# A hybrid decoder layer on one core: two token blocks turned on VectorE, token scales sent through DRAM, one weight split moved

## The chip, the cores and the metric

The kernel runs on one core of one Trainium2 chip. A core has TensorE (PE, with its weight loads PEld), VectorE (DVE), ScalarE (ACT), GpSimd (POOL) and SyncE (SP), each with its own in-order queue; SP issues nearly all the DMAs here, and 16 DMA engines carry them out. The metric is the device time of one execution in microseconds (us). All arithmetic is float32, with matmuls in three passes over operands that are split in a high and a low part (`fp32r`).

## What is computed

One decoder layer over 1024 tokens of width 1024, with a mixer of two kinds of heads and a feed-forward part:

```
h = rmsnorm(x, mix_pre_norm)
proj = h @ w_in
q_a, k_a, v_a, q_h, f_h, i_h, g_h = split(proj)
attn = rmsnorm(dilated_mixture_attention(q_a, k_a, v_a, slopes), attn_out_norm)
rec = hgrn2_recurrence(q_h, f_h, i_h, g_h, lower_bounds, hgrn_out_norm)
x = x + rmsnorm(concat([attn, rec]) @ w_out, mix_post_norm)
h = rmsnorm(x, mlp_pre_norm)
x = x + rmsnorm(square(relu(h @ w_ff1)) @ w_ff2, mlp_post_norm)
```

The root mean square of a token is one number per token. The kernel therefore multiplies the unscaled, gain-weighted `x` with `w_in` and puts the token's scale (`rstd0`) on the products afterwards.

## The kernel before

The work around the change is the first 60 us. The token dimension is cut into eight blocks of 128 tokens (`xr0` to `xr7`), the width into eight slices of 128 (`k`). The order of the work is written out by hand: instructions stand on each engine in the order in which the code issues them, and SP issues DMAs in that order too. At most eight of SP's DMAs are under way at once, since each one reuses the semaphore of the DMA eight before it and waits for that one to land.

**Turning x.** Matmuls need `x` with the width on the partitions. `x_turn` (L284) transposes pieces of 128 by 128 on PE into PSUM (L289), then ACT writes the high part `hTh` with the gain as scale (L290) and DVE the low part `hTl` (L291). `x_mm` multiplies the turned pieces with the first head's two weight slabs `wig0` (i and gate columns), three passes each (L90 to L92), into four PSUM banks `pig_0` to `pig_3`, which hold the blocks in the pairs (0, 1), (2, 4), (3, 5), (6, 7). The main loop goes over groups of blocks: groups[2] is blocks 2 and 3, groups[3] is 4 and 5, groups[4] is block 6, groups[5] is block 7. While group `i` is multiplied, group `i + 1` is turned, so each slice `k` of loop step 3 has one transpose of block 6, and each slice of step 4 one of block 7.

**Token scales.** `squares` (L300) sums the squares of a block's tokens on ACT; `rsqrt_mean` (L82, L83) makes `rstd0` on POOL, for blocks 0 to 5 after step 3 and for blocks 6 and 7 after step 4. `ig_evac` (L263 on ACT, L264 on DVE) empties a bank and scales it: one block's `inat` on ACT, then its `gate` on DVE; the second `inat` of a bank waits for the first `gate`.

**The query weights.** `w_split` (L86 on ACT, L87 on DVE) takes the next raw slab from the stream of weights, splits it into `wh` and `wl`, and issues the load of a later slab. The first head's query slab is `raw2`, its forget slab `raw3`. In the kernel before, `raw2` is split after step 4, between the emptying of `pig_0` and of `pig_1`; `raw3` is split when all four banks are empty.

**The rows of scales.** Query and forget products have tokens on the free dimension, so they need the scales as a row, the same on every partition (`rrow`). `row_scale` (L302) makes 512 of them at a time: four transposes on PE of a broadcast column (L307), and a copy on ACT (L308). It is called for each half from `hgrn_qf`, behind the query matmuls `pm_q` of that half; then DVE multiplies `pm_q` by `rrow` (L441). The bank of `pm_q` is then free for the forget matmuls `pm_f`. `pm_q` and `pm_f` take their banks in turn from the two that held `pig_0` and `pig_1`.

Between `ig_evac` and L441, DVE also makes masks and bounds (L383 to L389), ACT loads another table and computes the sigmoid of the gates (L268), and DVE multiplies with it (L269).

A later part of the kernel (L1163, L1205) already loads pieces of 128 rows as squares of 32 by 32 and turns them with DVE's transpose.

Of the kernel before, what the change touches and what calls it, by code (L numbers as in the profile page):

```python
# [8 lines left out]
F32 = mybir.dt.float32  # L9
F32R = mybir.dt.float32r  # L10
U8 = mybir.dt.uint8
AF = mybir.ActivationFunctionType
ALU = mybir.AluOpType
# [4 lines left out]
P = 128  # L18
T = 1024
D = 1024  # L20
NK = D // P
# [11 lines left out]
def f32(ap):  # L33
    return ap.bitcast(F32)
# [3 lines left out]
def hymba_layer(ctx, tc, x, w_in, w_out, w_ff1, w_ff2, g_pre, lb_logits, g_mix, g_post,  # L38
                g_mlp, g_mlp_post, bias_tab, level_masks, ident_in, fold_in, out):
    nc = tc.nc  # L40
    V, S, G, TE = nc.vector, nc.scalar, nc.gpsimd, nc.tensor
# [8 lines left out]
    dp = ctx.enter_context(tc.tile_pool(name="spill", bufs=1, space=DRAM))  # L50

    def slab(tag, name, dtype=F32, shape=(P, T)):
        return sp.tile(list(shape), dtype, tag=tag, name=name,
                       bufs={"S": 9, "T": 9, "P": 3, "BT": 2, "V8": 2, "R": 1}[tag])

    def bank(tag, name):
        return ps.tile([P, 512], F32, tag=tag, name=name,
                       bufs={"mm": 2, "s": 2, "t": 2, "pv": 2}[tag])
# [4 lines left out]
    def col(name, n=1):  # L63
        return tp.tile([P, n], F32, tag=f"c{n}", name=name)

    ident = cp.tile([P, P], F32, name="ident")
    own = cp.tile([P, 6, 32], U8, name="own")
    near = cp.tile([P, 3, 32], U8, name="near")
    gpre = cp.tile([P, NK], F32, name="gpre")
# [5 lines left out]
    rstd0 = cp.tile([P, NT], F32, name="rstd0")  # L75
# [4 lines left out]
    def rsqrt_mean(dst, ssum, n, width):  # L80
        t = col("ms", width)
        G.tensor_scalar(t, ssum, 1.0 / n, EPS, op0=ALU.mult, op1=ALU.add)  # L82
        G.tensor_tensor(out=dst, in0=t, in1=nhalf[:, :width], op=ALU.pow)  # L83

    def split_into(hi, lo, src, eng=V):
        S.activation(hi, src, AF.Copy)  # L86
        eng.tensor_tensor(out=lo, in0=src, in1=f32(hi), op=ALU.subtract)  # L87

    def three_pass(dst, lhs, rhs, start, stop):
        TE.matmul(dst, lhs[0], rhs[0], start=start, stop=False)  # L90
        TE.matmul(dst, lhs[0], rhs[1], start=False, stop=False)  # L91
        TE.matmul(dst, lhs[1], rhs[0], start=False, stop=stop)  # L92
# [10 lines left out]
    def w_load():  # L103
        i = done[0]
        if i < len(stream):
            raws[i] = wp.tile([P, T], F32, tag="raw", name=f"raw{i}", bufs=2)
            nc.sync.dma_start(out=raws[i], in_=stream[i][0])
            done[0] += 1

    def w_split(eng=V):  # L110
        i = done[1]
        if i < len(stream):
            if done[0] <= i:
                w_load()
            hl = stream[i][1]
            if hl is None:
                hl = (wp.tile([P, T], F32R, tag="wh", name=f"wh{i}", bufs=2),
                      wp.tile([P, T], F32R, tag="wl", name=f"wl{i}", bufs=2))
            else:
                hl = hl()  # L120
            raw = raws.pop(i)
            if WO0 <= i < W10:
                gain = gcols[:, i - WO0:i - WO0 + 1]
                S.activation(hl[0], raw, AF.Copy, scale=gain)
                eng.scalar_tensor_tensor(hl[1], raw, gain, f32(hl[0]), op0=ALU.mult, op1=ALU.subtract)
            else:
                split_into(hl[0], hl[1], raw, eng)
            parts[i] = hl
            done[1] += 1
            w_load()  # L130
# [95 lines left out]
    def part_tok(blk, k, t0, n=1):  # L226
        c = (t0 % 4) * P
        return tuple(blk[q, k // 4, t0 // 4][:, k % 4, c:c + n * P] for q in "hl")
# [8 lines left out]
    def x_load(t):  # L237
        nc.sync.dma_start(out=xrows[t], in_=x[t * P:(t + 1) * P, :])
# [4 lines left out]
    x_load(0)  # L243
    for _ in range(2):
        w_load()
    for t in range(1, NT):
        x_load(t)
    V.memset(f32(ones), 1.0)
    V.memset(nhalf, -0.5)
    rrow = slab("R", "rrow")  # L250
# [5 lines left out]
    pick32 = cp.tile([P, 32], F32, name="pick32")  # L256
    mix_dram = dp.tile([T, AW], F32, name="mixd")
    rec_dram = dp.tile([T, AW], F32, name="recd")
    x2_dram = [dp.tile([P, D], F32, name=f"x2d{t}") for t in range(NT)]

    def ig_evac(hd, pm, blocks):
# [21 lines left out]

    def x_turn(t0, n, k):  # L284
        hi, lo = part_tok(hT, k, t0, n)
        pt = bank("t" if turned[0] % 2 else "s", f"xt{t0}_{k}")[:, :n * P]
        turned[0] += 1
        for j in range(n):
            TE.transpose(pt[:, j * P:(j + 1) * P], xrows[t0 + j][:, k * P:(k + 1) * P], ident)  # L289
        S.activation(hi, pt, AF.Copy, scale=gpre[:, k:k + 1])  # L290
        V.scalar_tensor_tensor(lo, pt, gpre[:, k:k + 1], f32(hi), op0=ALU.mult, op1=ALU.subtract)  # L291

    def x_mm(t0, n, k):
        for t in range(t0, t0 + n):
            three_pass(place[t], part_tok(hT, k, t), ig_view(wig[0], k), k == 0, k == NK - 1)
# [4 lines left out]
            S.activation(dump, xrows[t], AF.Square, accum_out=ssq0[:, t:t + 1])  # L300

    def row_scale(hf):  # L302
        sl = slice(hf * 512, hf * 512 + 512)
        pt = bank("t", f"rb{hf}")
        for j in range(4):
            t = hf * 4 + j
            TE.transpose(pt[:, j * P:(j + 1) * P], rstd0[:, t:t + 1].to_broadcast([P, P]), ident)  # L307
        S.activation(rrow[:, sl], pt, AF.Copy)  # L308

    def keep_warm(n, w=256):  # L310

# [46 lines left out]
    for i, grp in list(enumerate(groups))[1:]:  # L358
        for k in range(NK):
            if i == 2 and k < LAG:  # L360
                x_turn(*grp, NK - LAG + k)
            if i == 1 and k < LAG:
                x_turn(*grp, NK - LAG + k)
            if i == 1 and k >= LAG:
                x_turn(*groups[2], k - LAG)
            elif 1 < i < len(groups) - 1:
                x_turn(*groups[i + 1], k)
            x_mm(*grp, k)
            if i in (2, 3) and k % 3 == 1:
                squares(3 * (i - 2) + k // 3, 1)  # L370
        if i == 3:
            rsqrt_mean(rstd0[:, :6], ssq0[:, :6], D, 6)
        if i == 4:
            ig_evac(heads[0], pms0[0], PAIRED[0])
            w_split()
            ig_evac(heads[0], pms0[1], PAIRED[1])
            squares(6, 2)
            rsqrt_mean(rstd0[:, 6:], ssq0[:, 6:], D, 2)
    for q in (2, 3):
        ig_evac(heads[0], pms0[q], PAIRED[q])  # L380
    w_split()
# [48 lines left out]
    def hgrn_qf(h):  # L430
        hd = heads[h]
        box = [None]
        w = w_get(4 * h + 2)
        qt = hd["qt"] = slab("S", f"qt{h}")
        sig = slab("P", f"sig{h}")
        for hf in range(2):
            sl = slice(hf * 512, hf * 512 + 512)
            yield from proj_t(w, f"q{h}", hf, box)
            if h == 0:
                row_scale(hf)  # L440
            V.tensor_tensor(out=qt[:, sl], in0=box[0], in1=rrow[:, sl], op=ALU.mult)  # L441
            S.activation(sig[:, sl], qt[:, sl], AF.Sigmoid)
            V.tensor_tensor(out=qt[:, sl], in0=qt[:, sl], in1=sig[:, sl], op=ALU.mult)
            yield 650.0
        w = w_get(4 * h + 3, 0)
        hd["prod"] = prod = [slab("BT", f"pr{q}{h}", F32R) for q in "hl"]
        kt = hd["kt"] = slab("S", f"kt{h}")
        tot = hd["tot"] = slab("S", f"tot{h}")
        for hf in range(2):
            sl = slice(hf * 512, hf * 512 + 512)  # L450
            for n, cost in enumerate(proj_t(w, f"f{h}", hf, box)):
                if hf == 0 and n == 3:
                    w_get(4 * h + 3, 2 if h + 1 < HH else 1)
                yield cost
            fr = half(f"fr{h}{hf}")
            V.tensor_tensor(out=fr, in0=box[0], in1=rrow[:, sl], op=ALU.mult)
            S.activation(tot[:, sl], fr, AF.Sigmoid)
            S.activation(kt[:, sl], fr, AF.Sigmoid, scale=-1.0)
            V.tensor_scalar(tot[:, sl], tot[:, sl], omlb[:, h:h + 1], lb[:, h:h + 1], op0=ALU.mult, op1=ALU.add)
            V.tensor_scalar(kt[:, sl], kt[:, sl], omlb[:, h:h + 1], None, op0=ALU.mult)  # L460
            full = half(f"pr{h}{hf}")
            V.tensor_tensor(out=full, in0=qt[:, sl], in1=kt[:, sl], op=ALU.mult)
            S.activation(prod[0][:, sl], full, AF.Copy)
            V.tensor_tensor(out=qt[:, sl], in0=qt[:, sl], in1=tot[:, sl], op=ALU.mult)
            V.tensor_tensor(out=prod[1][:, sl], in0=full, in1=f32(prod[0][:, sl]), op=ALU.subtract)
            if h == HH - 1 and hf == 0:
                rrow_by_class(0)
            yield 650.0
# [925 lines left out]
    for s in range(n_steps):  # L1394
        hd, i = divmod(s, 8)
# [18 lines left out]
        kind, g = ITEMS[i]  # L1414
# [746 lines left out]
    scale, base = gpre, lbl.rearrange("p h l -> p (h l)")  # L2161
# [95 lines left out]
    for i in range(4):  # L2257
        t = 4 + i
# [15 lines left out]
        lo, hi = slice(0, 256), slice(256, 512)  # L2274
# [84 lines left out]
```

## Time and profile before

| | |
|---|---|
| median of 3 runs | 1188.24 us (1188.04 to 1188.32) |
| the profiled execution | 1189.14 us |
| its span, from the first to the last instruction | 1187.1 us |
| granted TensorE clock, mean | 0.998 |
| PE busy | 1176.2 us, 99% of the span |
| DVE busy | 845.5 us, 71% |
| ACT busy | 549.6 us, 46% |
| moved by DMA | 175.50 MB, 148 GB/s |

The profile shows one execution. Times in its rows are us from the start of the span. A timeline row has the start, the duration, the engine, the line, the operation, output and inputs by the program's names without numbers (so `pig` is any of the four banks), shapes, how many were merged into the row, and in brackets the idle time before it and what ended it. The chain that ended last is followed back from the last instruction: at each step to what released it. Busy times of PE overlap, since matmuls are pipelined: how fast PE goes is read from the distance of two starts.

### The profile page before, as it was taken

The page shows a single profiled execution, that of the slowest core. Times are in us where ns is not written, and L with a number is a line of the kernel's source. Part 1 is how long each engine was busy: PE and PEld are TensorE (multiplying, and loading weights), DVE is VectorE, ACT ScalarE, POOL GpSimd, SP SyncE. Part 2 cuts the span into 40 slices and gives each one's busy share as a digit, 9 for nine tenths or more (in the row PEclk, how much of TensorE's full clock was granted, in tenths as well). Part 3 has the DMA queues.
Part 4 walks back from the last instruction along what each step waited for, and adds up shares of the span by engine and source line. Part 5 has one row for each costly group of instructions (what it writes and reads, how often), then busy time and mean ns, then how long its engine had stood idle before and what let it go on. Part 6 is the DMA issues. An engine that isn't in the chain of part 4 may idle for free.

```text
span 1187.1 us, 17573 instructions
## 1 busy us (share of the span) xinstructions
PE 1176.2 (99%) x6454; PEld 1002.0 (84%) x6454; DVE 845.5 (71%) x1436; ACT 549.6 (46%) x1082; POOL 294.5 (25%) x282
## 2 busy tenths in 40 slices
PE   9999999999999999999999999999999999999997
PEld 9898989878888888888888888888888888888886
DVE  5696969686766678587697676675686653588796
ACT  7633334343566677765654222222244544434562
POOL 0112122001111110252503775657540000000022
PEclk9999999999999999999999999999999999999999
DMA  5222323137454555472425465554587524433337
GB/s 221 68 68 89 98 86 98 49 102 183 117 137 103 157 133 138 118 220 100 169 90 204 159 221 184 182 177 169 194 331 271 178 89 157 162 94 101 110 104 284
DMA packets 106774, 175.50 MB, mean 148 GB/s; under 512 B 31680, under 2 KB 59712, under 8 KB 106688
## 3 DMA queue, kind: packets, MB, share of 16 engines
q1 hardware_dynamic: 106544, 174.37, 46.4%
q8 instruction: 51, 0.84, 0.3%
q14 instruction: 35, 0.29, 0.1%
q10 hardware_dynamic: 144, 0.00, 0.0%
HBM read 116.91 MB, written 47.99 MB: 139 GB/s over the span
## 4 chain that ended last, share of the span: by engine, by line
PE 90%; DVE 4%; ACT 3%; issue 1%; POOL 0%; DMA 0%; DVEq 0%; POOLq 0%; ACTq 0%
PE f L2099 18%; PE f2s L2099 7%; PE pig L90 2%; PE pig L92 2%; PE pig L91 2%; PE pwo L90 2%; PE pwo L92 2%; PE pwo L91 2%; PE pm_ak L90 1%; PE pm_ak L92 1%; PE pl L537 1%; PE pm_ak L91 1%; PE pm_av L90 1%; PE pm_av L92 1%; PE pm_q L90 1%
## 5 line engine op out<-in xcount | busy, mean ns | idle before, releaser
L87 DVE TENSOR_TENSOR al<-ar,ah 128x1024 fp32r<-128x1024 f32 x56 | 70.6, 1262 | 80.7 <-ACT ah L86 78.4
L2099 PE MATMUL f<-bh,ah 128*128 128x512 f32 x320 | 124.5, 389 | 0.0
L2099 PE MATMUL f<-bl,ah 128*128 128x512 f32 x320 | 124.5, 389 | 0.0
L2099 PE MATMUL f<-bh,al 128*128 128x512 f32 x320 | 124.5, 389 | 0.0
L86 ACT ACTIVATE ah<-ar 128x1024 fp32r<-128x1024 f32 x56 | 59.2, 1056 | 86.8 <-DMA ar<-actd 86.4
L2099 PEld LDWEIGHTS f<-bh,ah 128*128 128x128 f32 x320 | 60.1, 188 | 12.6
L2099 PEld LDWEIGHTS f<-bl,ah 128*128 128x128 f32 x320 | 60.1, 188 | 12.5
L2099 PEld LDWEIGHTS f<-bh,al 128*128 128x128 f32 x320 | 60.1, 188 | 12.3
L2173 POOL TENSOR_SCALAR lbl<-ssq 128x1 f32<-128x1 f32 x4 | 3.3, 820 | 245.8 <-ACT fd L2169 245.6
L1722 POOL TENSOR_TENSOR e<-x,e 128x512 f32<-128x512 f32 x14 | 21.6, 1542 | 130.9 <-DVE x L1673 123.7
L2099 PE MATMUL f2s<-bh,al 128*128 128x512 f32 (+1 forms) x128 | 48.9, 382 | 0.0
L2099 PE MATMUL f2s<-bl,ah 128*128 128x512 f32 (+1 forms) x128 | 48.9, 382 | 0.0
L2099 PE MATMUL f2s<-bh,ah 128*128 128x512 f32 (+1 forms) x128 | 48.9, 382 | 0.0
L711 POOL TENSOR_SCALAR tout<-traw 128x256 f32<-128x256 f32 x16 | 18.9, 1180 | 101.1 <-DMA traw<-in_bias_tab_dram 98.5
L87 DVE TENSOR_TENSOR bl<-br,bh 128x1024 fp32r<-128x1024 f32 x32 | 40.1, 1254 | 0.6 <-ACT bh L86 0.5
L2116 ACT ACTIVATE acc<-f 128x512 f32<-128x512 f32 x28 | 16.7, 598 | 49.4 <-PE f L2099 49.4
L86 ACT ACTIVATE bh<-br 128x1024 fp32r<-128x1024 f32 x32 | 33.6, 1050 | 3.6 <-PE f L2099 2.3
L759 POOL TENSOR_TENSOR kl<-kf,kh 64x512 fp32r<-64x512 f32 x12 | 16.2, 1353 | 74.8 <-ACT kh L758 71.3
L90 PE MATMUL pwo<-woh,mt 128*128 128x512 f32 x80 | 32.2, 403 | 0.0
L87 DVE TENSOR_TENSOR wl<-raw,wh 128x1024 fp32r<-128x1024 f32 x21 | 25.7, 1224 | 8.6 <-ACT wh L86 8.6
L92 PE MATMUL pwo<-woh,mt 128*128 128x512 f32 x80 | 31.3, 391 | 0.0
L91 PE MATMUL pwo<-wol,mt 128*128 128x512 f32 x80 | 31.2, 390 | 0.0
(1727 smaller groups left out, 3886.5 us busy)
## 6 DMA issues: line engine op xcount, KB each, us to landing
ar<-actd SPq DMA_DIRECT2D x56, 512.0 KB, 3.6
br<-in_w_ff_dram SPq DMA_DIRECT2D x16, 1024.0 KB, 6.1
raw<-in_w_in_dram SPq DMA_DIRECT2D x28, 512.0 KB, 4.1
w1r<-in_w_ff_dram SPq DMA_DIRECT2D x14, 1024.0 KB, 6.4
actd<-e SPq DMA_DIRECT2D x17, 768.0 KB, 4.2
actd<-e SPq DMA_DIRECT2D x11, 1024.0 KB, 4.1
xr<-in_x_dram SPq DMA_DIRECT2D x8, 512.0 KB, 8.4
raw<-in_w_out_dram SPq DMA_DIRECT2D x8, 512.0 KB, 4.5
```

The lines of the kernel that those rows point to most:

```text
L86: S.activation(hi, src, AF.Copy)
L87: eng.tensor_tensor(out=lo, in0=src, in1=f32(hi), op=ALU.subtract)
L90: TE.matmul(dst, lhs[0], rhs[0], start=start, stop=False)
L91: TE.matmul(dst, lhs[0], rhs[1], start=False, stop=False)
L92: TE.matmul(dst, lhs[1], rhs[0], start=False, stop=stop)
L537: TE.matmul(pl[a:b, n, :96], kt[:, (4 * u + n) * P + a:(4 * u + n) * P + b], qs[:, :, 32 * g:32 * g + 32], start=True, stop=True, skip_gro ...
L711: G.tensor_scalar(by_class(dst[:, part_ * w:(part_ + 1) * w]), in_blocks(raw[:, FAR * DIL:]), 8.0, None, op0=ALU.mult)
L759: G.tensor_tensor(out=kl[a:b], in0=src, in1=f32(kh[a:b]), op=ALU.subtract)
L1722: eng[0].tensor_tensor(out=e1[:, 3], in0=a21, in1=e1[:, 2], op=ALU.add)
L2099: TE.matmul(pm, a[:, j, c], b[:, j, d], start=start and j == 0 and q == 0, stop=stop and j == 1 and q == 2, skip_group_check=True)
L2116: S.activation(acc_at(p, i), pm, AF.Copy)
L2173: G.tensor_scalar(base[:, t:t + 1], sums[j][:, t:t + 1], 1.0 / D, EPS, op0=ALU.mult, op1=ALU.add)
```

## The change

It has three parts.

- Blocks 6 and 7 of `x` are loaded a second time, each by four DMAs, into `xsq6` and `xsq7`, as squares: row `r` of square (a, k, g) is 32 numbers of `x`, 128 bytes, put on partition 32g + r. A `V.transpose` over 128 by 1024 turns every 32 by 32 square in place, after which the tile holds what the PE transposes of the block gave. `x_turn` for these two blocks then reads the tile instead of PSUM, and PE does nothing for it. The plain loads of blocks 6 and 7, which `squares` needs, come after the new loads on SP's queue.
- `row_scale` no longer uses PE and ACT: one DMA writes 512 scales to DRAM, a second reads them back as a row on every partition. It is called when the scales are made, after steps 3 and 4.
- `w_split` of the query slab is called at the end of step 3, and no longer between the emptying of two banks after step 4.

```diff
+    SQUARED = (6, 7)
+    xsq = {t: slab("T", f"xsq{t}") for t in SQUARED}
     for t in range(1, NT):
+        if t in SQUARED:
+            src = x[t * P:(t + 1) * P, :].rearrange("(a r) (k g f) -> g r k a f", a=4, g=4, f=32)
+            for g in range(4):
+                nc.sync.dma_start(out=xsq[t][32 * g:32 * g + 32].rearrange("p (k a f) -> p k a f", k=NK, a=4), in_=src[g])
+        else:
+            x_load(t)
+    for t in SQUARED:
         x_load(t)
...
     def x_turn(t0, n, k):
         hi, lo = part_tok(hT, k, t0, n)
+        if t0 in SQUARED:
+            piece = xsq[t0][:, k * P:(k + 1) * P]
+            S.activation(hi, piece, AF.Copy, scale=gpre[:, k:k + 1])
+            V.scalar_tensor_tensor(lo, piece, gpre[:, k:k + 1], f32(hi), op0=ALU.mult, op1=ALU.subtract)
+            return
...
     def row_scale(hf):
-        sl = slice(hf * 512, hf * 512 + 512)
-        pt = bank("t", f"rb{hf}")
-        for j in range(4):
-            t = hf * 4 + j
-            TE.transpose(pt[:, j * P:(j + 1) * P], rstd0[:, t:t + 1].to_broadcast([P, P]), ident)
-        S.activation(rrow[:, sl], pt, AF.Copy)
+        nc.sync.dma_start(out=rstd_dram[hf].rearrange("(t p) -> p t", p=P), in_=rstd0[:, 4 * hf:4 * hf + 4])
+        nc.sync.dma_start(out=rrow[:, 512 * hf:512 * hf + 512], in_=rstd_dram[hf].partition_broadcast(P))
...
             x_mm(*grp, k)
+            if (i, k) in ((2, 6), (3, 2)):
+                V.transpose(xsq[4 + i], xsq[4 + i])
...
         if i == 3:
             rsqrt_mean(rstd0[:, :6], ssq0[:, :6], D, 6)
+            row_scale(0)
+            w_split()
         if i == 4:
             ig_evac(heads[0], pms0[0], PAIRED[0])
-            w_split()
             ig_evac(heads[0], pms0[1], PAIRED[1])
             squares(6, 2)
             rsqrt_mean(rstd0[:, 6:], ssq0[:, 6:], D, 2)
+            row_scale(1)
...
             yield from proj_t(w, f"q{h}", hf, box)
-            if h == 0:
-                row_scale(hf)
```

DVE's queue from block 7's low parts to the second weight split, before. In the names, `xt7_4` is slice 4 of block 7, `wl2` and `wl3` are the low parts of the query and the forget slab, and `pig0_1` is the bank `pig_1`:

```order
L291 SCALAR_TENSOR_TENSOR hTl11_96<-xt7_4_535,gpre_80,hTh11_95 128x128
L291 SCALAR_TENSOR_TENSOR hTl11_96<-xt7_5_542,gpre_80,hTh11_95 128x128
L291 SCALAR_TENSOR_TENSOR hTl11_96<-xt7_6_549,gpre_80,hTh11_95 128x128
L291 SCALAR_TENSOR_TENSOR hTl11_96<-xt7_7_556,gpre_80,hTh11_95 128x128
L264 TENSOR_SCALAR gate0_144<-pig0_0_145,rstd0_86 128x128 x2
L87 TENSOR_TENSOR wl2_568<-raw2_200,wh2_567 128x1024
L264 TENSOR_SCALAR gate0_144<-pig0_1_146,rstd0_86 128x128 x2
L264 TENSOR_SCALAR gate0_144<-pig0_2_147,rstd0_86 128x128 x2
L264 TENSOR_SCALAR gate0_144<-pig0_3_148,rstd0_86 128x128 x2
L87 TENSOR_TENSOR wl3_617<-raw3_202,wh3_616 128x1024
```

The same place now, from the first square transpose on:

```order
L381 STREAM_TRANSPOSE xsq6_118<-xsq6_118 128x1024
L306 SCALAR_TENSOR_TENSOR hTl11_96<-xt4_7_417,gpre_80,hTh11_95 128x256
L299 SCALAR_TENSOR_TENSOR hTl01_94<-xsq6_118,gpre_80,hTh01_93 128x128 x3
L381 STREAM_TRANSPOSE xsq7_119<-xsq7_119 128x1024
L299 SCALAR_TENSOR_TENSOR hTl01_94<-xsq6_118,gpre_80,hTh01_93 128x128
L299 SCALAR_TENSOR_TENSOR hTl11_96<-xsq6_118,gpre_80,hTh11_95 128x128 x4
L87 TENSOR_TENSOR wl2_507<-raw2_211,wh2_506 128x1024
L299 SCALAR_TENSOR_TENSOR hTl01_94<-xsq7_119,gpre_80,hTh01_93 128x128 x4
L299 SCALAR_TENSOR_TENSOR hTl11_96<-xsq7_119,gpre_80,hTh11_95 128x128 x4
L274 TENSOR_SCALAR gate0_155<-pig0_0_156,rstd0_86 128x128 x2
L274 TENSOR_SCALAR gate0_155<-pig0_1_157,rstd0_86 128x128 x2
```

The split `wl2` has moved from between the gates of two banks to ahead of block 7's eight low parts, and two transposes over 128 by 1024 have come into the queue. ACT's queue has moved alike: `wh2` stands between the squares of block 5 and block 7's eight high parts.

SP's queue from the load of block 5 on, now:

```order
L238 DMA xr5_107<-in_x_dram 128x1024
L252 DMA xsq6_118<-in_x_dram 32x32x32 x4
L252 DMA xsq7_119<-in_x_dram 32x32x32 x4
L238 DMA xr6_108<-in_x_dram 128x1024
L238 DMA xr7_109<-in_x_dram 128x1024
L261 DMA lbl_81<-in_lb_logits_dram 128x8
L262 DMA mraw_138<-in_level_masks_dram 128x448
L107 DMA raw2_211<-in_w_in_dram 128x1024
L107 DMA raw3_213<-in_w_in_dram 128x1024
L318 DMA rstdd_145<-rstd0_86 128x4x1
L319 DMA rrow_137<-rstdd_145 128x512
L107 DMA raw4_510<-in_w_in_dram 128x1024
```

The eight loads of squares are the second and third row; before, `xr6` stood directly behind `xr5`. The two DMAs of the first row half stand ahead of the load of `raw4` (half of the second head's `wig1`); those of the second half follow it, ahead of `raw5`.

More of the change, by code (lines that the diff above doesn't have):

```diff
@@ L258, in hymba_layer @@
     rec_dram = dp.tile([T, AW], F32, name="recd")
+    rstd_dram = dp.tile([2, 4 * P], F32, name="rstdd")
     x2_dram = [dp.tile([P, D], F32, name=f"x2d{t}") for t in range(NT)]
```

## Prediction

> **What bounds the kernel now.** I read the page first: the busy times, and the chain that ended last.
>
> ```profile
> PE 1176.2 (99%) x6454; PEld 1002.0 (84%) x6454; DVE 845.5 (71%) x1436; ACT 549.6 (46%) x1082; POOL 294.5 (25%) x282
> PE 90%; DVE 4%; ACT 3%; issue 1%; POOL 0%; DMA 0%; DVEq 0%; POOLq 0%; ACTq 0%
> ```
>
> PE carries 90% of the chain, DVE and ACT 7%, DMA none. So a microsecond less on PE counts, except where the chain leaves PE. All edits lie in the first 55 us, so I followed the chain there, in order of time.
>
> ```profile
> 34.80 0.12 PE xt L289
> 34.94 0.38 ACT hTh L290
> 35.34 0.35 DVE hTl L291
> 35.70 0.27 DVE gate L264
> ...
> 36.36 0.95 ACT wh L86
> 37.37 1.11 issue
> 38.48 0.35 DVE gate L264
> ...
> 39.12 2.19 ACT sq L300 x4
> ...
> 41.67 0.71 POOL rstd L83
> ...
> 43.56 0.95 ACT wh L86
> ...
> 49.87 0.61 DVE qt L441
> 50.52 0.50 PE pm_f L90
> ```
>
> This is the part that decides. At 34.80 the chain leaves PE with block 7's last transpose, and it comes back only at 50.52, with the first forget matmul `pm_f`. In between lie the emptying of the banks, the query split `wh` with the wait for its DVE half (36.36 to 38.48), the squares, the second scales, the forget split and the masks. Only then does DVE read `pm_q` (L441) and free the bank for `pm_f`. PE is busy all that time, but it isn't what the end waits for. The waits of PE say the same with a small number, since PE has just enough work to cover the chain:
>
> ```profile
> PE pm_f L90 <- DVE qt L441: 0.3, 1, 0.3
> PEld pm_q L92 <- DVE wl L87: 0.4, 1, 0.4
> ```
>
> **The change part by part.** First what PE loses, from its timeline around the removed rows.
>
> ```profile
> 31.36 0.27 PE L289 MATMUL xt<-ident,xr 128*128 128x128 f32 x1
> 31.83 0.27 PE L289 MATMUL xt<-ident,xr 128*128 128x128 f32 x1
> ...
> 35.10 0.28 PE L90 MATMUL pig<-wig0h,hTh 128*128 128x256 f32 x1
> 35.45 0.28 PE L90 MATMUL pig<-wig0h,hTh 128*128 128x256 f32 x1
> ...
> 43.75 0.60 PE L307 MATMUL rb<-ident,rstd 128*128 128x128 f32 x4
> 44.10 0.48 PE L90 MATMUL pm_q<-hTh,wh 128*128 128x512 f32 x1
> ...
> 49.66 0.60 PE L307 MATMUL rb<-ident,rstd 128*128 128x128 f32 x4
> ```
>
> A slice with a transpose takes 0.47 (31.36 to 31.83), without one 0.35, so sixteen transposes are worth 16 x 0.115 = 1.84 us. The scales' transposes take 0.35 (43.75 to 44.10) and 0.86 (49.66 to 50.52, the 0.3 of waiting in it). The wait for `wl` is 0.4. The sum on PE is 3.45 us. With it PE would be at `pm_f` at 49.66 - 1.84 - 0.35 - 0.4 = 47.07 instead of 50.52. How much of that is kept depends on when DVE and ACT have the bank free.
>
> So the chain has to be built anew. These are ACT's rows at its start, then the durations of one operation by shape, then DVE's rows and one ACT row of the forget split.
>
> ```profile
> 24.60 1.05 ACT L300 ACTIVATE sq<-xr 128x1024 f32<-128x1024 f32 x1
> ...
> 25.64 0.62 ACT L290 ACTIVATE hTh<-xt,gpre 128x128 fp32r<-128x128 f32 x2
> ```
>
> ```profile
> L290 ACT ACTIVATE hTh<-xt,gpre 128x128 fp32r<-128x128 f32 x32 | 10.5, 366 | 5.9 <-PE xt L289 5.2
> L983 ACT ACTIVATE pd<-pd,stat 128x128 f32<-128x128 f32 x8 | 3.1, 391 | 1.0 <-DVE stat L930 1.0
> L1205 DVE STREAM_TRANSPOSE row<-row 128x512 f32<-128x512 f32 x4 | 2.8, 704 | 0.0
> ```
>
> ```profile
> 26.04 0.61 DVE L291 SCALAR_TENSOR_TENSOR hTl<-xt,gpre,hTh 128x128 fp32r<-128x128 f32 x2 [0.81 <-ACT hTh L290]
> 37.34 1.23 DVE L87 TENSOR_TENSOR wl<-raw,wh 128x1024 fp32r<-128x1024 f32 x1 [0.59 <-ACT wh L86]
> 41.59 0.35 DVE L264 TENSOR_SCALAR gate<-pig,rstd 128x128 f32<-128x128 f32 x1 [1.98 <-ACT inat L263]
> ```
>
> ```profile
> 43.46 1.05 ACT L86 ACTIVATE wh<-raw 128x1024 fp32r<-128x1024 f32 x1
> ```
>
> ACT begins block 6 at 25.64, as now, and no longer waits for PE's pace. From there its queue is full: eight high parts, three squares (blocks 3 to 5), `wh`. A high part from PSUM steps by 0.25 (0.62 for two less one of 0.37); from SBUF I add 0.03, the difference of the means 391 and 366: 0.28. A square with its read steps by 1.04 (24.60 to 25.64). So `wh` starts at 25.64 + 8 x 0.28 + 3 x 1.04 = 31.00 and ends at 32.05. DVE's `wl` steps by 1.14 (37.34 to 38.48): block 7's low parts run from 33.2, eight by 0.26 (0.61 for two), and the first gate of `pig_0` comes at 35.30. From the first gate of two banks to ACT's next other operation took 43.46 - 41.59 = 1.87, about 0.15 of it waiting for the scales (41.67 + 0.71 = 42.38). So ACT comes to the squares of blocks 6 and 7 at 35.30 + 1.72 = 37.0, where it came at 39.12. From there on the chain has the same steps as before: gain 2.1 us. The split leaving this stretch is worth the 2.1 us from 36.36 to 38.48; block 7's low parts end only 0.3 earlier, since `wl` now stands ahead of them. `pm_f` starts at 48.4; PE, which is there at about 47.4 (it waits some 0.3 for `pig_0`'s gates first), waits 1.0 us. Of the 3.45 us on PE, 1.35 are not kept. The copies L308 that ACT loses are worth nothing: ACT waits for L441 there.
>
> The square transposes are hidden. Over 1024 columns one takes 1.2 to 1.4 us, at most twice the 704 ns for 512. The first must start by about 24.2 to be done when ACT is at 25.64; the second by 30.4, before ACT reaches block 7 at 31.95. Beyond that, each microsecond costs one. What they wait for are the loads:
>
> ```profile
> 0.00:5.00 5.00, 3.39 (x9) 2.57 (x10) 0.13 (x3) 1.49 (x2) 0.69 (x6) 1.00 0.62 192
> 5.00:10.00 5.00, 5.00 (x28) 4.80 (x29) 3.99 (x12) 4.33 (x12) 0.00 (x0) 1.00 1.02 415
> 426.00:428.00 2.00, 2.00 (x12) 1.69 (x11) 1.07 (x5) 1.71 (x4) 0.00 (x0) 1.00 0.99 156
> ```
>
> ```profile
> erows<-recd SPq DMA_DIRECT2D x8, 128.0 KB, 3.2
> swd<-stat SPq DMA_DIRECT2D x8, 2.0 KB, 3.6
> gcols<-in_g_mix_dram SPq DMA_DIRECT2D x1, 4.0 KB, 5.6
> gpost<-in_g_post_dram SPq DMA_DIRECT2D x1, 512.0 KB, 3.8
> ```
>
> The windows' last columns are DMA share and GB/s. The queue has moved 0.96 + 2.08 = 3.04 MB at 10 us; the eight loads ahead of the squares are 4.19 MB, so they end at 12.8. Eight loads of just this form, `erows` (128 KB, pieces of 128 bytes), kept the DMA engines full at 156 GB/s from 426 to 428. So 1.05 MB take 6.7 us and end at 19.5, landed by 22: `xsq6`, being the first half, with some 5 us to spare, `xsq7` with 8. The loads pushed back (`xr6`, `xr7`, masks, `raw2`, 1.8 MB at 415 GB/s) end by 24; the first wanted is `raw2`, at 31.0. Price zero; at the row's other bound, 4-byte pieces, see the third rival.
>
> A rule speaks against such loads. The Trainium skill (VectorE: DVE Perf Modes, section "The three transpose paths") calls a plain DMA that transposes by strides 19 times slower than the hardware's own transposing DMA, and tells authors to turn 128 by 128 pieces on TensorE. By that rule the loads would take an estimated 48 us, and the sum would be a loss near 30 us. The row above measures 2.7 times the plain rate's time and not 19, for a load that keeps 32 numbers together, so I keep the row's price.
>
> The scales' way through DRAM: the second half is made at 42.38 - 2.1 = 40.3. A write of 512 pieces lies between `swd` (3.6) and `gcols` (5.6, pieces of 4 bytes too), the broadcast read is nearest to `gpost` (3.8, twice the size), its issue 0.4. I take 3.6 + 3.8 + 0.4: landed at 48.1. DVE's second L441 wants it at 49.7:
>
> ```profile
> 51.78 0.69 DVE L441 TENSOR_TENSOR qt<-pm_q,rrow 128x512 f32<-128x512 f32 x1
> ```
>
> 1.6 us to spare, price zero; at 5.6 twice, 2.2 us late. SP waits inside these pairs, with `raw4` and `raw5` queued behind; both are wanted only for `wig1`, behind this L441. The first half is made some 8 us before the second and wanted 2 us before it, so it has more room.
>
> **The sum.** 1189.14 of the profiled execution less 2.1 is 1187.0. The median of the runs lies 0.9 below the profiled one: 1188.24 - 2.1 = 1186.1. Steps of 0.25 to 0.30 for the sixteen short ones on ACT and DVE before the gate, and 0.2 for the transposes, put the gain at 1.4 to 2.8: 1185.4 to 1186.8. About 0.2% (2.4 us) is what a measurement can tell from no change here; the forecast is just inside, and a third of its range beyond.
>
> **The rivals.**
> 1. The chain on DVE and ACT is shorter than I build it, and PE keeps all that is taken from it: `pm_f` at 47.1, gain 3.45, 1184.8. For it: PE has 90% of the chain. Against it: between 34.80 and 50.52 the chain has no PE row.
> 2. The gain is eaten at the second row half. Landing 2.2 us late (both trips at `gcols`' 5.6), it holds DVE's L441 and all behind it: `wig1`'s split, the forget rows. At most the 2.1 us go: 1188.2. Against it: `swd`'s 3.6 and `gpost`'s 3.8.
> 3. The squares come late, and the kernel is slower. The place is DVE's second transpose, with block 6's remaining low parts behind it and PE's block 6 matmuls waiting. It decides when the 1.05 MB take more than 17.6 us (12.8 to 30.4), that is under 60 GB/s. At `gcols`' price per piece (5.6 us for 1024), 8192 pieces take 45 us and end at 57.6, 27 us late: 1213. Against it: `erows`. For it: these loads meet a full queue. This is where the skill's factor, in the paragraph above, would lead too.
>
> **How the numbers follow.** Forecast 62%, first rival 20%, second 10%, third 8%. Faster by over 0.2%: a third of the forecast and the first rival, 0.40. Slower: 0.08. Within 0.2%: the rest, 0.52. The range goes from the first rival's 1184.6 (0.2 below its time) to the second's 1188.3, and leaves out the third and some of the first; the forecast's own is 1185.4 to 1186.8.
>
> **What would show it.** Right: `pm_f`'s first matmul near 48.4, with a PE wait of about 1 us for L441; `wh` of the query slab at 31 and the two late squares at 37; DVE's transposes at 24.2 and 28, 1.2 us each, with no DMA wait ahead of them; `rrow`'s second half landed by 48. Wrong: `pm_f` near 47.1 (first rival); a DMA named as what L441 waits for (second); DVE idle before a transpose until an `xsq` DMA (third); a PE wait after 60 us that is new, which would mean that the 2.1 us are lost elsewhere.

## The result and the profile after

The changed kernel takes 1195.3 us (median of 6 runs, 1193.87 to 1195.46) against 1188.28 us before: a ratio of 1.0057, 95% interval 1.0046 to 1.0067. It is 7.0 us slower. The profiled execution took 1195.37 us with a span of 1193.2.

The chain that ended last, from the page of the changed kernel, has lost some of PE, DVE and ACT and gained DMA and "issue":

```profile
PE 88%; issue 4%; DVE 2%; ACT 2%; DMA 2%; POOL 0%; DVEq 0%; SPq 0%; POOLq 0%; ACTq 0%
```

The same chain between 32 and 60 us, in order of time (start, length, what), is one path through the two trips of the scales:

```profile
32.04 8.55 DMA rstdd<-rstd
...
41.08 0.37 SPq L107
...
41.55 12.46 DMA rstdd<-rstd
...
54.02 5.24 DMA rrow<-rstdd
...
59.35 0.70 DVE qt L454
```

A write of 2 KB (`rstdd<-rstd`) takes 8.55 us, the second one 12.46, and the read behind it (`rrow<-rstdd`) 5.24. Only at 59.35 can DVE read the second `pm_q` (L454), where it wanted to at 48.9. The waits, and TensorE's timeline around them, show what that does:

```profile
DVE qt L454 <- DMA rrow<-rstdd: 10.4, 1, 10.4
PE pm_f L90 <- DVE qt L454: 7.5, 2, 6.7
```

```profile
47.69 0.47 PE L90 MATMUL pm_f<-hTh,wh 128*128 128x512 f32 x1 [0.83 <-DVE qt L454]
...
53.02 0.39 PE L92 MATMUL pm_f<-hTh,wl 128*128 128x512 f32 x1
60.10 0.80 PE L90 MATMUL pm_f<-hTh,wh 128*128 128x512 f32 x1 [6.69 <-DVE qt L454]
60.69 0.63 PE L91 MATMUL pm_f<-hTl,wh 128*128 128x512 f32 x1
61.12 0.63 PE L92 MATMUL pm_f<-hTh,wl 128*128 128x512 f32 x1
...
68.53 0.28 PE L90 MATMUL pig<-wig1h,hTh 128*128 128x256 f32 x1
```

Before, the second row and what follows it began here:

```profile
56.10 0.39 PE L90 MATMUL pm_f<-hTh,wh 128*128 128x512 f32 x1
...
61.54 0.28 PE L90 MATMUL pig<-wig1h,hTh 128*128 128x256 f32 x1
```

The first `pm_f` row begins at 47.69, 2.83 us sooner than the 50.52 before. The next matmul would be due at 53.24, one step behind the last, but the second row can't begin until 60.10: 6.86 us later, of which TensorE is idle for 6.69. Then the first step is 0.59 and the next thirteen are 0.43 instead of 0.23, and the row takes 8.43 us instead of 5.44. So the first matmul of `wig1` comes at 68.53 where it came at 61.54 before: -2.83 + 6.86 + 2.99 = 7.0, which is the difference of the medians. (The two profiled executions end only 6.2 us apart, since that of the kernel before lay 0.9 above its median.) The slow steps are a lower granted clock (the column before the last two):

```profile
55.00:56.00 1.00, 0.00 (x0) 0.00 (x0) 0.00 (x0) 0.00 (x0) 0.00 (x0) 1.00 1.85 27
56.00:57.00 1.00, 0.00 (x0) 0.00 (x0) 0.00 (x0) 0.00 (x0) 0.00 (x0) 0.50 0.00 0
...
65.00:66.00 1.00, 1.00 (x4) 0.81 (x3) 0.66 (x2) 0.83 (x2) 0.00 (x0) 0.50 1.05 393
66.00:67.00 1.00, 1.00 (x6) 0.78 (x5) 0.97 (x2) 0.00 (x0) 0.00 (x0) 0.88 0.91 320
```

The write itself moves its data at once. In windows of the changed kernel the last two columns are DMA share and GB/s:

```profile
33.00:33.20 0.20, 0.20 (x3) 0.20 (x3) 0.20 (x2) 0.20 (x2) 0.00 (x0) 1.00 0.79 7
33.20:33.40 0.20, 0.20 (x4) 0.20 (x4) 0.20 (x2) 0.20 (x2) 0.00 (x0) 1.00 0.39 3
33.40:40.60 7.20, 7.20 (x42) 6.16 (x41) 3.45 (x12) 4.82 (x14) 1.59 (x3) 1.00 0.00 0
```

The packets of the first write, issued at 32.04, are gone by 33.4. Then no DMA moves anything until 40.6, when the write is reported complete. So 7.2 of the 8.55 us are neither transfer nor queue. Two theories stand from here. W: the write's form, many 4-byte pieces, is what is slow to complete. Q: any small trip through DRAM is late at this place, because of the queue and the loads in it.

### The profile page after: what moved, and what is told of

Read it like the earlier page. It is cut to its first block, busy times and chain, and to the rows that moved or that the text cites. A ratio compares the mean times of both kernels' runs of the same rounds, so it can differ in the third digit from the quotient of the medians.

```text
span 1193.2 us, 17548 instructions
## 1 busy us (share of the span) xinstructions
PE 1175.1 (98%) x6430; PEld 1000.3 (84%) x6430; DVE 846.1 (71%) x1438; ACT 547.7 (46%) x1080; POOL 296.0 (25%) x282
## 4 chain that ended last, share of the span: by engine, by line
PE 88%; issue 4%; DVE 2%; ACT 2%; DMA 2%; POOL 0%; DVEq 0%; SPq 0%; POOLq 0%; ACTq 0%
PE f L2112 18%; PE f2s L2112 7%; PE pig L90 2%; PE pig L91 2%; PE pig L92 2%; PE pwo L90 2%; PE pwo L92 2%; PE pwo L91 2%; DMA rstdd<-rstd 2%; PE pl L550 1%; PE pm_ak L90 1%; PE pm_ak L92 1%; PE pm_ak L91 1%; PE pm_av L90 1%; PE pm_av L92 1%
## 5 line engine op out<-in xcount | busy, mean ns | idle before, releaser
L2112 PE MATMUL f2s<-bh,al 128*128 128x512 f32 (+1 forms) x128 | 48.9, 382 | 0.0
L2112 PE MATMUL f2s<-bl,ah 128*128 128x512 f32 (+1 forms) x128 | 48.9, 382 | 0.0
L2112 PE MATMUL f2s<-bh,ah 128*128 128x512 f32 (+1 forms) x128 | 48.9, 382 | 0.0
L90 PE MATMUL pm_f<-hTh,wh 128*128 128x512 f32 x64 | 27.5, 429 | 7.5 <-DVE qt L454 7.5
```

The lines of the kernel that those rows point to most:

```text
L2112: TE.matmul(pm, a[:, j, c], b[:, j, d], start=start and j == 0 and q == 0, stop=stop and j == 1 and q == 2, skip_group_check=True)
```

## Experiments

### One part at a time

**rows_only**: the kernel before, with the scales' way through DRAM alone (`row_scale` itself is that of the changed kernel).

```
             rsqrt_mean(rstd0[:, :6], ssq0[:, :6], D, 6)
+            row_scale(0)
...
             rsqrt_mean(rstd0[:, 6:], ssq0[:, 6:], D, 2)
+            row_scale(1)
...
-            if h == 0:
-                row_scale(hf)
```

> The kernel before with one part of the change alone: the scales go through DRAM in pieces of 4 bytes (blocks 6 and 7 are turned on TensorE, the query split stays at its old place). Theory W: the second scales are made at 42.4; the write takes 8.5 to 12.5 us, the read 5.3, so the row lands between 56 and 60, where VectorE wants it at 51.8; the second pm_f starts at 57 to 61 instead of 56, and the time is 1 to 8 us above the one before, 1189.3 to 1196. Rival S (the loss needs the square loads, whose packets crowd the queues): 1187 to 1188.3, since TensorE is rid of 1.2 us.

Measured: 1195.26 us, ratio 1.0061 (1.0049 to 1.0074). DVE's wait for the row and TensorE's wait behind it are there without any square load:

```profile
DVE qt L438 <- DMA rrow<-rstdd: 8.6, 1, 8.6
PE pm_f L90 <- DVE qt L438: 6.1, 2, 4.9
```

Rival S is out: this part alone costs what the whole change costs.

**squares_only** and **split_only**: the other two parts, each alone, with the scales on TensorE; **pe_rows**: both together (the changed kernel with the old `row_scale` put back at its old place, which the cut shows).

```
     def row_scale(hf):
-        nc.sync.dma_start(out=rstd_dram[hf].rearrange("(t p) -> p t", p=P), in_=rstd0[:, 4 * hf:4 * hf + 4])
-        nc.sync.dma_start(out=rrow[:, 512 * hf:512 * hf + 512], in_=rstd_dram[hf].partition_broadcast(P))
+        pt = bank("t", f"rb{hf}")
+        for j in range(4):
...
+        S.activation(rrow[:, sl], pt, AF.Copy)
```

> The kernel before with the square loads and their transposes on VectorE alone; rows on TensorE, query split at its old place. Theory: TensorE is at the first pm_f 1.84 us sooner (48.4 to 48.7), and the chain, without the wait for TensorE's pace, some 1.8 us sooner too: 1186.2 to 1186.6. Rival (the chain does not move while the split stands in it): 1187.8 to 1188.3.

> The kernel before with the query split's new place alone. Theory (TensorE keeps its sixteen transposes and both row transposes, so that it has little to give): the chain would allow 2.1 us, TensorE only its wait for wl of 0.4 and the 0.3 for the evacuation: 1187.5 to 1187.9. Rival (the chain alone sets the end): 1186.2.

> The row of token scales goes back to TensorE (transposes at the two old places); squares and the earlier split stay. Theory W (the 7 us are lost only in the row's way through DRAM): DVE's first q evacuation ends near 47.5 as after the change, TensorE is there at 46.9 + 0.35 + 0.6 = 47.9, the first pm_f starts at 47.9 to 48.2 and the second follows without a gap: 2.3 to 2.6 us less than before, 1185.7 to 1186.0. Rival S (the squares or the split have a part in the loss): 1188.3 or more.

Measured: the squares alone 1186.36 us, 0.9986 (0.9977 to 0.9995); the split alone 1188.89, 1.0006 (0.9997 to 1.0015); both 1186.28, 0.9984 (0.9975 to 0.9992), a little above the expected 1185.7 to 1186.0. The squares and their transposes on VectorE are the whole gain. The split gives nothing, and its expectation of a small gain failed. TensorE's timeline in split_only shows why:

```profile
35.34 0.33 PE L289 MATMUL xt<-ident,xr 128*128 128x128 f32 x1 [1.50 <-DVE hTl L291]
```

With the split ahead of block 7's parts, DVE comes late to the banks of the transposes, and TensorE waits 1.5 us for a bank that it did not wait for before. With the squares that bank is not needed, so the wait is gone, but the gain of the split is then only 0.3 us on the chain: the first q evacuation starts at 46.90 in pe_rows and at 47.22 in squares_only.

### What makes the write slow

**forms**: eight forms of a small write on an empty queue, ahead of the first load.

```
+    def try_write(name, shape, view, source, rd):
+        d = dp.tile(shape, F32, name=f"wr_{name}")
+        nc.sync.dma_start(out=view(d), in_=source)
+        r = rd(d)
+        nc.sync.dma_start(out=back[:r.shape[0], :r.shape[1]], in_=r)
...
+        try_write(f"blocks{n}", [4, P], lambda d: d.rearrange("t p -> p t"), src4, lambda d: d[:, :16])
```

> The kernel before, with sixteen small writes to DRAM ahead of its first load, one after the other on an otherwise empty queue, eight forms twice; each is followed by a small read that waits for it, so that the time from issue to completion shows. Its total time means nothing. Theory W1 (the number of 4-byte pieces sets it): 512 pieces of 4 bytes take about 8.5 us however far apart they lie, 256 about 5, 128 about 3.3; 128 pieces of 16 bytes at most 3.6. Theory W2 (neighbouring pieces that share a stretch of DRAM are written one behind the other): 512 pieces that lie 64 or 512 bytes apart take at most 4 us, and neighbouring ones 8.5. Rival Q (the queue with its traffic): every form takes 2 to 4 us on the empty queue, the 512 neighbouring pieces too.

SP's timeline, second round. Each write's time is the start of the read behind it (L251) less its own start (L249):

```profile
41.52 0.38 SPq L249 DMA_DIRECT2D wr_blocks<-ident  x1
49.70 0.25 SPq L251 DMA_DIRECT2D back<-wr_blocks  x1
...
53.28 0.42 SPq L249 DMA_DIRECT2D wr_one<-ident  x1
60.67 0.23 SPq L251 DMA_DIRECT2D back<-wr_one  x1
...
71.87 0.38 SPq L249 DMA_DIRECT2D wr_gap_of_row<-ident  x1
73.88 0.26 SPq L251 DMA_DIRECT2D back<-wr_gap_of_row  x1
74.18 0.57 SPq L249 DMA_DIRECT2D wr_owner_gap<-ident  x1
78.40 0.56 SPq L251 DMA_DIRECT2D back<-wr_owner_gap  x1
79.00 0.48 SPq L249 DMA_DIRECT2D wr_rows<-ident  x1
80.58 0.25 SPq L251 DMA_DIRECT2D back<-wr_rows  x1
```

The change's form (`wr_blocks`) takes 8.2 us here too, with nothing else in the queue (10.8 in the first round, where it is the very first DMA): rival Q is out. But the number of pieces isn't it either: 128 pieces of 4 bytes side by side (`wr_one`) take 7.4, and 512 pieces 512 bytes apart take 2.0 (64 bytes apart: 2.8). Theory W1 falls and W2's times hold: what is slow is that small pieces lie close to each other. It doesn't need pieces from different partitions: in `wr_owner_gap` each partition writes four numbers of its own, 8 bytes apart, and that takes 4.2 (3.4 in the first round).

**sweep**: how near they must lie.

```
...
+        for step, tag in ((1, "a"), (2, "b"), (4, "c"), (8, "d"), (16, "e"), (32, "f")):
+            try_write(f"one_{tag}{n}", [P, step], lambda d: d[:, :1], ident[:, :1], lambda d: d[:16, :1])
...
```

> The kernel before, with twenty small writes to DRAM one after the other on an empty queue ahead of its first load (ten forms twice), each with a small read that waits for it; the total time means nothing. First six forms: one number (4 bytes) of each of the 128 partitions, 4, 8, 16, 32, 64 and 128 bytes apart; then runs of 8, 16, 32 and 64 bytes side by side. Theory W3 (pieces in one stretch of 64 bytes are completed one behind the other, some 0.4 us each): 7.5, 4.4, 2.8, 2.0, 1.6, 1.6 us, and for the runs 4.4, 2.8, 2.0, 1.6. Theory W4 (the stretch is larger, 512 bytes): the times stay long beyond 64 bytes and fall only at 512. Theory W5 (only pieces of exactly neighbouring addresses collide): 7.5 for the first form, under 2.5 for all the spaced ones.

The DMA issues of this kernel (the last number is the us from issue to landing; a to f are 4, 8, 16, 32, 64 and 128 bytes apart, the run is 16 bytes side by side):

```profile
wr_one_a<-ident SPq DMA_DIRECT2D x2, 0.5 KB, 7.1
...
wr_one_b<-ident SPq DMA_DIRECT2D x2, 0.5 KB, 4.4
...
wr_one_c<-ident SPq DMA_DIRECT2D x2, 0.5 KB, 3.3
...
wr_one_d<-ident SPq DMA_DIRECT2D x2, 0.5 KB, 1.5
...
wr_one_f<-ident SPq DMA_DIRECT2D x2, 0.5 KB, 1.5
...
wr_run_c<-ident SPq DMA_DIRECT2D x2, 2.0 KB, 1.7
```

The time falls by steps with the distance and is at its floor from 32 bytes on. That is the shape of W3, with a floor at 32 bytes instead of 64. But W3 gave runs of 16 bytes side by side the same 2.8 us as single numbers 16 bytes apart, and they take 1.7 against 3.3: the length of a piece counts beside its distance. So W3's rule, pieces completed one behind the other, is not shown, and neither is what in the memory's path makes it so. The Trainium skill (DMA: Bandwidth & Descriptors, section "Specifications") says that a transfer below 512 bytes is a read, a change and a write back. That doesn't price this case by itself: pieces of 4 bytes at a distance of 32 cost 1.5 us, as little as at 128.

**pieces16**: the change, with the scales written as 128 pieces of 16 bytes and the row kept in that order.

```
-        nc.sync.dma_start(out=rstd_dram[hf].rearrange("(t p) -> p t", p=P), ...
+        nc.sync.dma_start(out=rstd_dram[hf].rearrange("(p t) -> p t", p=P), ...
...
-            V.tensor_tensor(out=qt[:, sl], in0=box[0], in1=rrow[:, sl], op=ALU.mult)
+            V.tensor_tensor(out=by_block(qt[:, sl]), in0=by_block(box[0]), in1=spread_rows(hf), op=ALU.mult)
```

> The scales still go through DRAM, but are written as 128 pieces of 16 bytes (one for each partition) and read back in that order; VectorE and ScalarE read the row with a stride. Theory W (the write of 512 pieces of 4 bytes is what is late): the second write takes at most 3.5 us as the small writes of four neighbouring numbers did later in the kernel, so the second row has landed by 39.5 + 3.5 + 0.4 + 5.3 = 48.7, the second pm_f follows the first with a gap under 0.6 us, and the time is 1185.2 to 1186.2. Rival Q (any small trip through DRAM at this place is late, whatever its pieces, since it stands in SP's queue with the weight loads): the write lands 8 to 12 us after its issue again, and the time is 1194 to 1196.

Measured: 1187.87 us, 0.9996 (0.9988 to 1.0005). The second write stands at the same place of SP's order and takes 1.41 us instead of 12.46. The first one takes 1.45 (32.19 to 33.64), so that its read and the load of `raw4` are done before the second write comes, and it meets an empty queue (SP's timeline):

```profile
39.60 0.32 SPq L318 DMA_DIRECT2D rstdd<-rstd  x1
41.01 0.32 SPq L319 DMA_DIRECT2D rrow<-rstdd  x1
```

The 7 us come back with it, but not the rest of the gain: the total missed its expectation by 1.7 us. The multiplications that read the row with a stride of 16 bytes have grown, in all heads, as this kernel's groups show; the same operation takes 0.69 us in the changed kernel:

```profile
L460 DVE TENSOR_TENSOR qt<-pm_q,rrow 128x512 f32<-128x512 f32 x8 | 8.5, 1061 | 9.6 <-PE pm_q L92 9.6
```

That they are what costs the 1.7 us was not tested alone; **turned**, below, reads the row without a stride and is 1.9 us faster.

**late_raw**: the change, with the load of `raw4` behind the second trip.

```
+            hold[0] = True
             w_split()
+            hold[0] = False
...
             row_scale(1)
+            w_load()
```

> The changed kernel, but the load of 512 KB that SP issues between the two trips of the scales is issued behind the second one. Theory W (the second write's 12.5 us are 5.5 in the queue behind the first row's read and this load, and 7 for its own completion): without the load the queue has only 256 KB ahead of it, the second write takes 8.5 to 9.5 us, the second row lands 3 to 4 us sooner, near 55.7, the idle of TensorE falls from 6.7 to about 3.3, and the time to between 1188.8 (clock not halved) and 1192.3 (still halved). Rival V (the second write is slower for a reason of its own): lands at 59 again, 1195.

Measured: 1193.83 us, 1.0044 (1.0029 to 1.0059), 1.5 us below the change; the expected 3 us or more did not come. SP's timeline:

```profile
41.75 0.39 SPq L321 DMA_DIRECT2D rstdd<-rstd  x1
52.66 0.32 SPq L322 DMA_DIRECT2D rrow<-rstdd  x1
```

The second write takes 10.9 us instead of 12.46. So the load has a share of about 1.5. The rest of the queue's share is the first row's read: issued at 41.33, it moves between 43 and 46, and the write's packets come behind it. In the changed kernel the write's last packets, behind read and load, are gone only at 47.2, 5.65 us after its issue, where the first write took 1.36. So the queue's share is some 4.3 us, and then the write takes 6.8 more, as the first one took its 7.2.

### What the wait does to TensorE

**warm**: the change, with 12 matmuls on zeros (24 instructions) between the two forget rows.

```
+            if h == 0 and hf == 1:
+                wb = bank("pv", "warm")
+                for _ in range(12):
+                    TE.matmul(wb[:, :256], zero.to_broadcast([P, P]), zero.to_broadcast([P, 256]), start=True, stop=True)
```

> The changed kernel with 12 matmuls on zeros, whose result nobody reads, between the two forget rows, so that TensorE isn't idle there. The wait for the second row stays: the second pm_f starts at 60.1. If the rest of the loss is the halved clock (matmul steps of 0.43 instead of 0.227 for 6.1 us after the wait), those 24 matmuls take 5.5 instead of 8.4 us and the time falls by 2.7 to 3.0, to 1192.3 to 1192.6. If the slow steps come from something else (DMA traffic, late operands), the time stays at 1195.3.

Measured: 1194.07 us, 1.0045 (1.0030 to 1.0061), 1.2 below the change. TensorE's timeline and one of its waits:

```profile
53.16 5.39 PE L467 MATMUL warm<-zero 128*128 128x256 f32 x24
59.68 0.50 PE L90 MATMUL pm_f<-hTh,wh 128*128 128x512 f32 x1 [1.13 <-DVE qt L454]
...
65.26 0.28 PE L90 MATMUL pig<-wig1h,hTh 128*128 128x256 f32 x1
```

```profile
PE pl L554 <- DVE kt L583: 0.9, 1, 0.9
```

The cause of the slow steps is the idle: with the filler the granted clock stays at 1.00, and the second row takes 5.58 us (59.68 to 65.26) instead of 8.43. But of these 2.9 us less than half arrives at the end, and not the expected 2.7 to 3.0, since TensorE then meets DVE's own late work, as at `pl`. The row also begins 0.4 us sooner here, with a second write of 12.12 us. So of the 7.0 us lost, at most 1.2 hang on the clock, and the rest on the late row.

### Repairs

**turned**: VectorE turns the scales in 32 by 32 squares ahead of the write, so that the pieces are 128 bytes long and the row keeps its old order; **turned_masks**: with it, DVE's work on the masks moved ahead of the query split; **masks**: that move on pe_rows, with the rows on TensorE. In the two turned versions the calls also come later: the first behind the late squares, the second behind the emptying of the last bank.

```
...
+        V.transpose(rturn, rstd32)
+        for g in range(4):
+            nc.sync.dma_start(out=rstd_dram[hf].rearrange("(t g i) -> g t i", t=4, g=4)[g],
+                              in_=rturn[32 * g + 4 * hf:32 * g + 4 * hf + 4])
         nc.sync.dma_start(out=rrow[:, 512 * hf:512 * hf + 512], in_=rstd_dram[hf].partition_broadcast(P))
```

> The scales go through DRAM, but VectorE turns them first in 32 by 32 squares (one small operation a half, in gaps before the next weight split), so that they are written as sixteen pieces of 128 bytes, four small writes a half, and the row is read back in its old order without a stride. Theory W (what is slow is neighbouring small pieces in one stretch of DRAM): each write is complete 1.6 to 3 us after its issue, the second row lands by 49, the pm_f rows follow without a long gap, first pm_f at 47.7, and no VectorE operation gets longer: 1185.2 to 1185.7, below the version with the rows on TensorE. Rival Q (small trips through DRAM at this place are slow as such): 1190 or more.

> As the version with turned scales, and VectorE's work on the masks (six small operations and the difference for lb, 1.5 us) moved from behind the forget split to before the query split, where VectorE was idle for 1.6 us. The forecast's claim that the chain on VectorE and ScalarE, not TensorE, sets the start of pm_f: VectorE is at the first q evacuation 1.4 us sooner (near 45.4), TensorE no longer waits the 0.8 us, pm_f starts at 46.9, and the time falls by a further 0.7 to 0.9, to 1184.4 to 1185.0. Rival P (TensorE's own work sets it, the wait shown is no real one): no change against the version without this move.

> Squares, early split, rows on TensorE, and the work on the masks moved ahead of the query split as in the version that took 1185.0. There the move was worth 1.0 us with the rows off TensorE. Theory (with the row transposes on it TensorE itself sets the start of pm_f, no wait for VectorE is left in the version without the move): VectorE is ready 1.4 us sooner and nothing follows, 1186.0 to 1186.4. Rival (the chain on VectorE and ScalarE sets it here too): 1185.2 to 1185.4.

Measured: turned 1186.0 us, 0.9981 (0.9973 to 0.9990), somewhat above its expectation; turned_masks 1185.0, 0.9972 (0.9960 to 0.9983), the fastest of all and faster than both kernels of the change; masks 1186.01, 0.9983 (0.9974 to 0.9992). In turned the second half's four writes are done in 2.15 us, and neither they nor the read hold anybody any longer (SP's timeline), and TensorE waits for the first evacuation alone:

```profile
41.26 1.25 SPq L323 DMA_DIRECT2D rstdd<-rturn  x4
43.41 0.34 SPq L325 DMA_DIRECT2D rrow<-rstdd  x1
```

```profile
47.77 0.47 PE L92 MATMUL pm_f<-hTh,wh 128*128 128x512 f32 x1 [0.81 <-DVE qt L460]
```

In turned_masks DVE's evacuation comes at 45.53 and `pm_f` starts without a wait:

```profile
45.53 0.68 DVE L460 TENSOR_TENSOR qt<-pm_q,rrow 128x512 f32<-128x512 f32 x1
```

```profile
46.77 0.39 PE L92 MATMUL pm_f<-hTh,wh 128*128 128x512 f32 x1
```

So with the rows off TensorE the chain on DVE and ACT sets the start, and 1.0 us was to be had there. With the rows on TensorE (masks) the same move gives 0.3 at most, within the intervals: there TensorE itself is the bound. For that reason pe_rows and turned end within 0.3 us of each other, too: in the one TensorE makes the rows, in the other it waits 0.8 us for DVE.

## Why the prediction was wrong

**The step that failed** is the second term of the scales' way through DRAM: "I take 3.6 + 3.8 + 0.4: landed at 48.1". The write took 12.46 us, the read 5.24, and the row landed at 59.3, 11.2 us late: 8.9 by the write, 1.4 by the read, 1.2 by the start (41.55 instead of 40.3), less the 0.4 for the issue. Three things were wrong in it. The lower end, `swd<-stat`, has the same 2 KB, but it is written as 128 pieces of 16 bytes, the form that took 1.4 to 1.5 us in pieces16, 1.7 in the sweep and up to 2.9 in forms. The upper end, `gcols`, has pieces of 4 bytes, but it is a read; no write of 4-byte pieces was among the rows. And the queue was counted only for those behind the trips. The second scales were made at 39.43, sooner than forecast, but the first trip held SP from 32 to 40.6, so that their write was issued at 41.55 and then stood some 4.3 us behind the first row's read and `raw4`. Why the read took 5.24 was not tested; between 55 and 56 the DMA engines are busy at 27 GB/s, and from 56 to 57 nothing moves (the windows in the first section). The first half had little room as well: its row landed near 46.0, 0.9 us ahead of its use at 46.85.

**The second rival** named the right place and mechanism, and the sign that it named came: a DMA is what L454 waits for. Its price was capped wrongly: "At most the 2.1 us go". A wait is not limited by the gain that it follows; here it went on through an idle TensorE (6.7 us) and a halved clock. With one in ten for it, and 2.2 us as its size, the range stopped at 1188.3.

**The chain** held. The forecast had `wh` at 31.0, the late squares at 37.0 and `pm_f` at 48.4, with 1.0 us of waiting; measured are 30.17, 36.18, 47.69 and 0.83:

```profile
30.17 1.05 ACT L86 ACTIVATE wh<-raw 128x1024 fp32r<-128x1024 f32 x1
...
36.18 1.05 ACT L315 ACTIVATE sq<-xr 128x1024 f32<-128x1024 f32 x1
```

All three came 0.7 to 0.8 us sooner than forecast, and the difference stands at the first term already, `wh`. With a healthy trip (turned) the kernel takes 1186.0, beside the forecast of 1186.1, but that agreement is partly luck: `pm_f` starts there at 47.77, 2.75 us sooner than before and not 2.1, of which 2.3 arrive in the time, and the 2.1 us were credited to the wrong part (next paragraph). The first rival, that TensorE keeps all of its 3.45 us, needed one thing more: the masks out of the chain (turned_masks, 3.3 us below before).

**The split** was credited wrongly: "The split leaving this stretch is worth the 2.1 us". Alone it is worth nothing, and with the squares 0.3 on the chain and nothing measurable in time: it left one place of a full chain for another one of the same chain. It is the squares that shorten the chain: with them alone, and the split at its old place, the late squares of ACT start at 36.55 (squares_only), 2.6 us sooner than the 39.12 before.

**The squares** came in time, as forecast. DVE's transposes ran at 23.28 and 27.02, each in 1.2 us, and did not wait for a load:

```profile
23.28 1.23 DVE L381 STREAM_TRANSPOSE xsq<-xsq 128x1024 f32<-128x1024 f32 x1
```

The third rival did not come, nor did the estimated 48 us by the factor 19 of the Trainium skill (VectorE: DVE Perf Modes, section "The three transpose paths"): the kernel with the squares alone is 1.8 us faster.

## What to carry to other kernels

A DMA that the trace does not show is priced by a row with the same pieces in the same direction, their length and their distance, and not by its kilobytes; a scatter of single numbers from many partitions into one row of DRAM is to be suspected, and turning it first, so that each partition writes a run of 32 numbers, costs one operation of 0.2 us. When a trip like that ends in front of a wait, its lateness is not bounded by what the change gains, so a rival built on it needs a price without a cap. Moving a piece of work within a chain that has no slack gains nothing; moving it into an idle stretch of its engine did (1.0 us).

## What the runs showed of the hardware

- A write to DRAM of 128 pieces of 4 bytes, on an empty queue, is complete 1.5 us after its issue if they lie 32 bytes or more apart, 3.3 us at 16 bytes, 4.4 at 8, and 7.1 at 4 (sweep). Runs of 16 bytes side by side take 1.7. Its packets can have left long before: by 33.4 in the changed kernel, completion at 40.6.
- A VectorE multiplication of 512 numbers whose second operand is read at steps of 16 bytes takes 1.06 us instead of 0.69.
- The granted clock fell to 0.50 at 56.0, 2.6 us after the end of TensorE's last matmul, and came back at about 66.2, 6.1 us after it had work again. In rows_only the two times were 5.1 and 3.7 us, in late_raw 2.2 and 4.2. The Trainium skill (TensorE: Matmul & The Clock Gate, section "Part 1: The HAM clock gate") gives windows of some 3.4 us for both and calls them free-running; the halving agrees, the times here lie on both sides of that.
